# A feed-forward block by seven half products in place of eight

## The chip, the core and the metric

One NeuronCore of a Trainium2 chip runs the whole program. The metric is the device time of one execution in microseconds (us). The kernel is written in Python with one instruction stream for each engine: TensorE (PE, matmuls), VectorE (DVE), ScalarE (ACT), GpSimd (POOL) and SyncE (SP, which issues the transfers).

## The reference

Three residual blocks, one behind the other, on an input of 1024 rows and 1024 columns in fp32. The change touches the second block's end and the third block. The end of the second:

```python
    x = x + jnp.concatenate([y_rwkv, y_conv], axis=-1) @ w_out[l]
    h = rmsnorm(x, norm_mlp_g[l])
    x = x + jnp.square(jax.nn.relu(h @ w_ff1[l])) @ w_ff2[l]
return rmsnorm(x, norm_final_g)
```

`w_ff1` has 1024 x 4096 elements, `w_ff2` 4096 x 1024. The third block, cut to its products:

```python
proj = rms_norm_3(x, g_pre) @ w_in
u_a, v_a, z_a, q_b, k_b, v_b, z_b, gate_a, gate_b = jnp.split(proj, SPLIT_OFFS, axis=-1)
y_a = spatial_gating(jax.nn.gelu(u_a), jax.nn.gelu(v_a), ln_g, ln_b, w_s, b_s) * jax.nn.silu(z_a)
y_b = mixture_of_dilations(q_b, k_b, v_b) * jax.nn.silu(z_b)
m = sigmoid(gate_a + b_gate[:1024]) * (y_a @ w_pa) + sigmoid(gate_b + b_gate[1024:]) * (y_b @ w_pb)
return x + rms_norm_3(m @ w_o, g_post)
```

## The kernel before

**Split products.** Every fp32 operand of a matmul is split into a high part and the rest (`split`, L179: an ACT copy for the high part at L183, a DVE subtraction for the low one at L184), and each product is three matmuls, high by high, high by low and low by high (`mm3`, L255, the matmul at L261; with a tile of weights or of activations on the stationary side, 512 columns moving). A unit of weights is loaded into a buffer of the pool `wp` and split there (`wunit`, L222). Activations stand transposed in halves of 512 rows (`act_half`, L193), in slots of a ring of six buffers of 32 KB per partition.

**The feed-forward** (`feed_forward`, L1679). The hidden width of 4096 is cut into 16 units of 256. `first` makes a unit's hidden values for 512 rows at a time, 24 matmuls for 128 hidden columns, relu on ACT, square and split; `second` (L1705) multiplies a unit by its 256 rows of `w_ff2` and adds the 1024 x 1024 result into `xm` in SBUF (L1711 on DVE). Each layer has 16 x 96 = 1536 matmuls of 512 columns. The hidden values never leave SBUF. Beside the last units the final norm of the second block (`rms_rows`, L1666) and the first of the third (`rms_T`, L197) run tile by tile, then `vb_proj` begins.

**Seven products** (`Seven`, L1728). In the third block a 1024 x 1024 product of activations with a unit of 256 columns is taken as a 2 x 2 matrix of blocks by 2 x 2 blocks of weights, with seven block products in place of eight and sums ahead and behind. `sums` (L1744) makes the sums of activation blocks in four steps, each with four additions of high and low part (L1753) and four further operations (L1755 to L1758), all on POOL; `last_sum` (L1764) splits the fourth. `run` (L1779) goes through the units: four loads of 256 KB of raw weights, three differences of weights on POOL (L1795, the tile T), seven splits into tiles w (eight buffers, five products ahead), twelve matmuls per product (L1813) into the PSUM tags a, b and d, and five additions on DVE (L1835 to L1846). Its users are 16 `Gated` units and 8 `Gate` units. A Gated unit's `prepare` (L2118 to L2128) loads and normalizes v and loads the tile ws; its `begin` transposes ws on PE (L2133).

**Order.** A scheduler sets the order of each engine's instructions from the program's order, priorities and the pools' buffers; pools that stand at the same addresses in SBUF make the later one's first writer wait for the earlier one's last reader. SP issues all transfers, in one queue. `weave` and `woven` take turns between generators; `wunit_in` (L241) loads the tail's first weights `wx` while the last Gate units run. In the tail (`merge`, L2201) `from_b` makes the second product, `from_a` the first.

Of the kernel before, what the change touches and what calls it, by code (L numbers as in the profile page):

```python
# [55 lines left out]
class Ctx:  # L56
# [184 lines left out]
    def wunit_in(self, p, a, new):  # L241

        nc = self.nc
        hi, lo = (p.tile([128, 8, 256], R, name=self.nm("wx")) for _ in range(2))
# [1434 lines left out]
def feed_forward(c, X, xm, p):  # L1679

    nc, ins = c.nc, c.ins
    w1, w2 = ins["w_ff1_2"][0], ins["w_ff2_2"][0]
    unit = lambda u: slice(256 * u, 256 * u + 256)
    act = {}

    def first(u, W, hf):
        hs = slice(512 * hf, 512 * hf + 512)
        ah, al = act[u]
        for i in range(2):
            q = c.cm(W, slice(128 * i, 128 * i + 128), X, hf)  # L1690
            r = p.tile([128, 512], F32, tag="fr", name=c.nm("fr"), bufs=1)
            nc.scalar.activation(r, q, AF.Relu)
            nc.vector.tensor_tensor(r, r, r, op=OP.mult)
            c.split(ah[:, i, hs], al[:, i, hs], r)
            yield

    def load1(u):
        act[u] = tuple(p.tile([128, 2, 1024], R, tag=t, name=c.nm(t), bufs=2) for t in ("ah", "al"))
        return c.wunit([w1[:, unit(u)]])

    W = [load1(u) for u in range(2)]
    for hf in range(2):
        for u in range(2):
            yield from first(u, W[u], hf)
    def second(u, W, tiles):  # L1705
        for t in tiles:
            for nh in range(2):
                q = c.psum("mm")
                ns = slice(512 * nh, 512 * nh + 512)
                c.mm3(q, act[u], W, slice(128 * t, 128 * t + 128), ns, [(0, 0), (1, 1)])  # L1710
                nc.vector.tensor_tensor(xm[t][:, ns], xm[t][:, ns], q, op=OP.add)  # L1711
            yield

    load2 = lambda u: c.wunit([w2[unit(u), :]], ktiles=2)
    for u in range(14):
        yield from second(u, load2(u), range(8))
        W = load1(u + 2)
        for hf in range(2):
            yield from first(u + 2, W, hf)

    W = [load2(u) for u in (14, 15)]
    for hf in range(2):
        for u in range(2):
            yield from second(14 + u, W[u], range(4 * hf, 4 * hf + 4))

class Seven:  # L1728
# [15 lines left out]
    def sums(self, tmp):  # L1744
# [3 lines left out]
        self.s4 = tmp.tile([128, 4, 512], F32, name="sum4")  # L1748
        for k in range(4):
            v = {}  # L1750
            for n, (h, l) in ((21, self.A21), (22, self.A[4]), (11, self.A[1]), (12, self.A[2])):
                v[n] = tmp.tile([128, 512], F32, tag="v%d" % n, name=c.nm("v"), bufs=1)
                TT(v[n], h[:, k].bitcast(F32), l[:, k].bitcast(F32), op=OP.add)  # L1753
# [16 lines left out]
    def load(self, u, p):  # L1770

        c, nc = self.c, self.c.nc
        r = p.tile([128, 4, 4, 128], F32, tag="raw", name=c.nm("raw"), bufs=2)
        a, b = u.parts
        for i, (w, k) in enumerate(((a, 0), (b, 0), (b, 1), (a, 1))):
            nc.sync.dma_start(r[:, i], w[512 * k:512 * k + 512].rearrange("(k p) n -> p k n", p=128))
        return r

    def run(self, units, rp, p, st):  # L1779
        c, nc = self.c, self.c.nc  # L1780
        N = len(units)
        order = [(0, 1), (0, 2), (0, 6)]
        for n in range(N):
            order += [x for x in ((n, 2), (n, 5), (n, 7), (n + 1, 1), (n, 4), (n + 1, 6), (n, 3)) if 0 < x[0] < N or n == x[0] and x[1] != 2]
        for u in units[:1]:
# [716 lines left out]
```

## Time and profile before

| | |
|---|---|
| median of 3 runs | 3922.23 us (3918.51 to 3922.97) |
| the profiled execution | 3905.47 us |
| its span, first to last instruction | 3903.7 us |
| PE busy | 3718.5 us, 95% |
| DVE busy | 2178.6 us, 56% |
| ACT busy | 1316.1 us, 34% |
| POOL busy | 803.4 us, 21% |
| moved by DMA | 354.14 MB, mean 91 GB/s |

Busy shares are means over the span. The clock is the one granted to TensorE, as a share of full speed. An idle time of an engine other than the one that sets the end costs nothing. "L261" is line 261 of the kernel above.

### The profile page before, as it was taken

To read this page: it belongs to the slowest core of one execution; us is meant where nothing else is said; L and a number is where in the kernel's file an instruction comes from. 1 tells how busy PE (TensorE), PEld (TensorE's weight loads), DVE (VectorE), ACT (ScalarE), POOL (GpSimd) and SP (SyncE) were. 2 spreads that over 40 slices of the span, in tenths; PEclk is the share of its full clock that TensorE was granted. 3 is DMA by queue.
4 is the path that set the end of the run, shared out by engine and by line. 5 is a ranking of instruction groups with operands and counts; after the bars stand their busy time and mean duration, and the time that the engine had idled before them with its cause. 6 is when DMAs were issued, how large, how long until landed. Compare 5 with 4: busy or idle time off the path is not lost.

```text
span 3903.7 us, 53217 instructions
## 1 busy us (share of the span) xinstructions
PE 3718.5 (95%) x20000; PEld 3076.6 (79%) x20000; DVE 2178.6 (56%) x4701; ACT 1316.1 (34%) x2683; POOL 803.4 (21%) x1161
## 2 busy tenths in 40 slices
PE   7999999799979989999999999999989999998998
PEld 6788788687867778888888878878777888887887
DVE  5356568768977855444444644444442666544443
ACT  4444435642234334221122233333321333332322
POOL 1011124400048620000000001111150655420000
PEclk9999998899989999999999999999999999999999
DMA  5321242341212232111111132111122333337462
GB/s 148 126 64 51 73 148 70 128 134 60 89 56 52 62 113 92 54 54 44 45 53 44 71 107 66 44 49 55 49 96 86 93 102 105 102 119 249 152 228 94
DMA packets 362948, 354.14 MB, mean 91 GB/s; under 512 B 54014, under 2 KB 288322, under 8 KB 362690
## 3 DMA queue, kind: packets, MB, share of 16 engines
q1 hardware_dynamic: 362690, 350.73, 28.5%
q8 instruction: 158, 2.59, 0.3%
q14 instruction: 100, 0.82, 0.1%
HBM read 263.63 MB, written 82.31 MB: 89 GB/s over the span
## 4 chain that ended last, share of the span: by engine, by line
PE 83%; DVE 5%; POOL 4%; DMA 4%; ACT 2%; issue 1%; SPq 1%; DVEq 0%; POOLq 0%; ACTq 0%
PE mm L261 57%; PE b L1813 5%; PE d L1813 3%; PE a L1813 3%; PE s L1964 2%; DMA wraw<-in_w_in_dram 1%; PE s L542 1%; PE t L578 1%; PE o L1986 1%; DVE ws L748 1%; PE s L2156 1%; PE o L2038 1%; POOL v L1753 1%; PE t L213 1%; PE o L588 1%
## 5 line engine op out<-in xcount | busy, mean ns | idle before, releaser
L261 PE MATMUL mm<-ahi,whi 128*128 128x512 f32 x1936 | 762.4, 395 | 12.6 <-ACT whi L183 11.6
L261 PE MATMUL mm<-alo,whi 128*128 128x512 f32 x1936 | 760.6, 393 | 1.6 <-DVE alo L218 1.6
L261 PE MATMUL mm<-ahi,wlo 128*128 128x512 f32 x1936 | 759.1, 393 | 2.5 <-DVE wlo L184 2.5
L183 ACT ACTIVATE whi<-wraw 128x1024 fp32r<-128x1024 f32 (+2 forms) x266 | 268.7, 1055 | 671.2 <-DMA wraw<-in_w_ff_dram 320.9
L184 DVE TENSOR_TENSOR wlo<-wraw,whi 128x1024 fp32r<-128x1024 f32 (+2 forms) x266 | 322.0, 1247 | 257.5 <-PE mm L261 198.9
L261 PEld LDWEIGHTS mm<-ahi,whi 128*128 128x128 f32 x1936 | 366.9, 190 | 90.1 <-issue 12.4
L261 PEld LDWEIGHTS mm<-ahi,wlo 128*128 128x128 f32 x1936 | 365.8, 189 | 78.7 <-DVE wlo L184 3.3
L261 PEld LDWEIGHTS mm<-alo,whi 128*128 128x128 f32 x1936 | 366.4, 189 | 76.6 <-DVE alo L218 2.5
L261 PE MATMUL mm<-whi,ahi 128*128 128x512 f32 (+2 forms) x960 | 351.6, 371 | 31.8 <-ACT go L2097 10.9
L261 PE MATMUL mm<-wlo,ahi 128*128 128x512 f32 (+2 forms) x960 | 352.1, 367 | 0.0
L261 PE MATMUL mm<-whi,alo 128*128 128x512 f32 (+2 forms) x960 | 350.5, 366 | 1.6 <-DVE alo L218 1.6
L1711 DVE TENSOR_TENSOR xm<-xm,mm 128x512 f32<-128x512 f32 x256 | 173.9, 686 | 119.0 <-PE mm L261 118.6
L261 PEld LDWEIGHTS mm<-whi,ahi 128*128 128x128 f32 x960 | 183.8, 192 | 63.9 <-ACT go L2097 12.2
L261 PEld LDWEIGHTS mm<-wlo,ahi 128*128 128x128 f32 x960 | 183.8, 191 | 30.2 <-issue 3.8
L261 PEld LDWEIGHTS mm<-whi,alo 128*128 128x128 f32 x960 | 183.1, 191 | 31.0 <-issue 2.5
L261 PE MATMUL mm<-whi,ah 128*128 128x512 f32 x512 | 202.3, 395 | 0.0
L261 PE MATMUL mm<-wlo,ah 128*128 128x512 f32 x512 | 202.1, 395 | 0.0
L261 PE MATMUL mm<-whi,al 128*128 128x512 f32 x512 | 202.1, 395 | 0.0
L207 POOL TENSOR_SCALAR x<-x,rT 128x1024 f32<-128x1024 f32 x16 | 20.9, 1306 | 753.9 <-PE mm L261 672.9
L1813 PE MATMUL b<-sum,w 128*128 128x512 f32 x576 | 147.1, 398 | 0.2 <-DVE w L184 0.2
L1180 DVE SCALAR_TENSOR_TENSOR cva<-cvh,vecs,cva 128x1022 f32<-128x1022 f32 (+29 forms) x120 | 145.4, 1262 | 0.2
L560 POOL TENSOR_SCALAR S<-S,sn 128x64 f32<-128x64 f32 (+8 forms) x96 | 56.5, 592 | 382.6 <-DVE sn L558 158.2
(623 smaller groups left out, 6900.3 us busy)
## 6 DMA issues: line engine op xcount, KB each, us to landing
wraw<-in_w_in_dram SPq DMA_DIRECT2D x33, 1024.0 KB
wraw<-in_w_ff_dram SPq DMA_DIRECT2D x32, 1024.0 KB
wraw<-in_w_out_dram SPq DMA_DIRECT2D x24, 1024.0 KB
raw<-in_w_in_dram SPq DMA_DIRECT2D x96, 256.0 KB
wraw<-in_w_proj_a_dram SPq DMA_DIRECT2D x16, 1024.0 KB
wraw<-in_w_in_dram SPq DMA_DIRECT2D x27, 512.0 KB
gv<-go SPq DMA_DIRECT2D x32, 256.0 KB
vl<-gv SPq DMA_DIRECT2D x16, 512.0 KB
```

The lines of the kernel that those rows point to most:

```text
L183: nc.scalar.activation(hi, src, AF.Copy)
L184: nc.vector.tensor_tensor(lo, src, hi.bitcast(F32), op=OP.subtract)
L213: nc.tensor.transpose(q[:, 128 * j:128 * j + 128], xn[:, (k + j) * 128:(k + j + 1) * 128], self.ident)
L261: nc.tensor.matmul(out, lhs[a][:, kl, ls], rhs[b][:, kr, rs], start=first and n == 0, stop=last and n == tot - 1)
L542: nc.tensor.matmul(q[:, :b - a], self.Q[0:64, h, qs], kl, start=False, stop=True)
L560: nc.gpsimd.tensor_scalar(S_[:, :n], S_[:, :n], r, 1.0, op0=OP.mult, op1=OP.mult)
L578: nc.tensor.transpose(t[:w, (2 * j + s) * 128:(2 * j + s + 1) * 128], Ps[s][:, k:k + w], c.ident)
L588: nc.tensor.matmul(o[:, :256], v[:w, 0:128], ph[:w, sl], start=first, stop=last, skip_group_check=True)
L1180: nc.vector.scalar_tensor_tensor(a[:, 30 - j:], h[:, 0:994 + j], wj, a[:, 30 - j:], op0=OP.mult, op1=OP.add)
L1711: nc.vector.tensor_tensor(xm[t][:, ns], xm[t][:, ns], q, op=OP.add)
L1813: nc.tensor.matmul(o, w[:, i, k], self.A[P][j][:, k], start=P in (1, 6, 5) and m == 0, stop=m == 11, skip_group_check=True)
L1964: nc.tensor.matmul(q[:, :256], qk[:, a, qcol], qk[:, b, kcol], start=n == 0, stop=n == 2)
```

## The change

The feed-forward is rewritten and takes both layers by seven block products (units 0 and 1 of the first layer by eight, `EIGHT = 2`). A hidden unit's four blocks (11, 12, 21, 22: half of the rows by half of the columns) come out of `Seven`; the class `Hidden` squares them, makes five sums on POOL and writes the seven operands (the five sums and the blocks 11 and 22) to `hS` in DRAM, 256 KB each. The class `Second` reads these and blocks of `w_ff2` back, 512 KB at a time, makes the sums of weights on POOL and takes the seven products in four groups, (5, 7), (4, 1), (3, 6) and (2), each in eight steps of 24 matmuls per product, accumulating in PSUM. At the end of a group the results are added to `C`, four tiles of 1024 columns per half, into which the residual was loaded from `xmid` in DRAM, where `rows` had stored it. The last group is woven with the first four tiles' norms.

`Seven` is cut into `plan`, `load`, `make`, `product`, `by_eight` and `run`, and the activation sums' first additions may run on DVE (`both=True`). In the third block the plan and the first loads stand ahead of `v_proj`, two splits are made within it, the transposes of ws are kept in program order, and a second unit of `from_b` runs on the PSUM tag a before the pools of the tail open.

```diff
-def feed_forward(c, X, xm, p):
...
-    def sums(self, tmp):
+    def sums(self, new, both=False):
 
         c, nc = self.c, self.c.nc
         TT = nc.gpsimd.tensor_tensor
+        T0 = nc.vector.tensor_tensor if both else TT
...
-                TT(v[n], h[:, k].bitcast(F32), l[:, k].bitcast(F32), op=OP.add)
+                T0(v[n], h[:, k].bitcast(F32), l[:, k].bitcast(F32), op=OP.add)
...
+    def by_eight(self, p):
+
+        c, e = self.c, self.eight
+        for i, (n, hf, col) in enumerate(self.order[:4 * e]):
+            while self.made < min(4 + 2 * i, 4 * e) or self.made < min(2 * i, 4 * e + 5):
+                self.make(p)
...
+            A = ((self.A[1], self.A[2]), (self.A21, self.A[4]))[hf]
+            for kh in range(2):
+                self.product(o, self.W[n, (col, kh)], A[kh], kh == 0, kh == 1)
+            self.units[n].result(hf, col, o)
+            yield
...
+class Hidden:
+
+    SUMS = {1: (11, 22, OP.add), 2: (21, 22, OP.add), 5: (11, 12, OP.add), 6: (21, 11, OP.subtract), 7: (12, 22, OP.subtract)}
...
+    def out(self, m, x):
+        self.c.nc.sync.dma_start(self.hS[m - 1, 128 * self.n:128 * self.n + 128], x)
+
+    def result(self, hf, col, x):
+        c, nc = self.c, self.c.nc
+        me = 11 + 10 * hf + col
+        if me == 11 or self.n < EIGHT:
+            o = self.new(me)
+            nc.scalar.activation(o, x, AF.Relu)
+            nc.vector.tensor_tensor(o, o, o, op=OP.mult)
+        else:
+            o = x
+            nc.vector.scalar_tensor_tensor(o, x, 0.0, x, op0=OP.max, op1=OP.mult)
+        self.x[me] = o
+        if me in (11, 22):
+            self.out({11: 3, 22: 4}[me], o)
+        for m, (a, b, op) in self.SUMS.items():
+            if m not in self.done and a in self.x and b in self.x:
+                self.done.add(m)
+                t = self.sc.tile([128, 512], F32, tag="sc", name=c.nm("sc"), bufs=4)
+                nc.gpsimd.tensor_tensor(t, self.x[a], self.x[b], op=op)
+                self.out(m, t)
...
+class Second:
...
+    def parts(self, group, s, tp):
...
+        for m in group:
+            for x in self.B[m][:2]:
+                if x not in B:
+                    i, j = x // 10 - 1, x % 10 - 1
+                    B[x] = self.raw(self.w2[i][:, 2 * s:2 * s + 2, 512 * j:512 * j + 512])
+        for m in group:
+            A = self.raw(self.hS[m - 1, 256 * s:256 * s + 256].rearrange("(k p) n -> p k n", p=128))
+            o = out[m] = c.slot([128, 4, 2, 512], R, "fop")
+            c.split(o[:, 0], o[:, 1], A)
+            b = B[self.B[m][0]]
+            if len(self.B[m]) > 1:
+                t = tp.tile([128, 2, 512], F32, tag="ft", name=c.nm("ft"), bufs=2)
+                nc.gpsimd.tensor_tensor(t, b, B[self.B[m][1]], op=self.B[m][2])
+                b = t
+            c.split(o[:, 2], o[:, 3], b)
+        return out
...
+            seven.plan(units, rp, [(w7, 6), (w2p, 2)], eight=EIGHT)
+            tt = enter("T")
+            first = seven.by_eight(tt)
+            weave([(islice(first, 4), 4), (staggered(map(tile, range(4, 8)), 2), 10)])
...
+            weave([(first, 4), (seven.sums(four, both=True), 12)])
+            seven.last_sum()
+            for _ in seven.run(tt, st):
+                pass
+        with pool("f4") as f4, pool("ft") as tp, pool("fe") as ep:
+            c.set_banks(mm=list(range(8)))
+            sec = Second(c, hS, w2)
+            with pool("f4x") as fx:
+                sec.raws = [(f4, 5)] * 5 + [(fx, 10)] * 10
+                C = []
+                r = sec.run([(5, 7), (4, 1), (3, 6)], tp, ep, C)
...
+                weave([(sec.run([(2,)], tp, ep, C), 8), (norms[0], 12)])
+                X.append(c.act_half())
+                weave([(islice(vb, 8), 8), (norms[1], 12)])
...
+                for i, _ in enumerate(woven([(b.v_proj(X, vp, new), 16), (seven.sums(lambda: [tmp.tile([128, 512], F32, tag="v%d" % i, name=c.nm("v")) for i in range(4)]), 12)])):
+                    if i == 24:
+                        seven.make()
+                        seven.make()
...
-            nc.tensor.transpose(q[:, 0:128], self.ws, c.ident)
+            c.tc.keep_in_program_order(nc.tensor.transpose(q[:, 0:128], self.ws, c.ident))
...
-                for _ in b.from_b(0, 0, first[0], Ab, "a", new):
-                    pass
+                w = c.slot([128, 2, 8, 256], R, "wx")
+                first.append(c.wunit_in((w[:, 0], w[:, 1]), c.ins["w_proj_b_3"][0][:, 256:512], new))
+                for u in range(2):
+                    for _ in b.from_b(u, 0, first[u], Ab, "a", new):
+                        pass
```

Line numbers in the rows of the order are those of the kernel they stand in. First SP, in the middle of the feed-forward before: a unit's weights per load, first and second layer in turn, each 1 MB.

```order
L233 DMA wraw_2965_16353<-in_w_ff2_2_dram 128x2x1024
L233 DMA wraw_2986_16491<-in_w_ff1_2_dram 128x8x256
L233 DMA wraw_2997_16619<-in_w_ff2_2_dram 128x2x1024
L233 DMA wraw_3018_16757<-in_w_ff1_2_dram 128x8x256
L233 DMA wraw_3029_16885<-in_w_ff2_2_dram 128x2x1024
```

SP after the change, where the second layer begins: sc are sums of the last hidden units on their way to DRAM, f4 the buffers that the second layer loads, numbered in the order of the program.

```order
L2431 DMA f4_3217_18067<-hS_14680 128x2x512
L2390 DMA hS_14680<-sc_3212_18019 128x512
L2431 DMA f4_3219_18074<-hS_14680 128x2x512
L2431 DMA f4_3222_18083<-in_w_ff2_2_dram 128x2x512
L2390 DMA hS_14680<-sc_3213_18036 128x512
L2390 DMA hS_14680<-sc_3214_18039 128x512
L2431 DMA f4_3250_18242<-hS_14680 128x2x512
L2431 DMA f4_3253_18299<-in_w_ff2_2_dram 128x2x512
L2431 DMA f4_3254_18301<-in_w_ff2_2_dram 128x2x512
L2431 DMA f4_3255_18303<-hS_14680 128x2x512
L2431 DMA f4_3223_18085<-in_w_ff2_2_dram 128x2x512
L2431 DMA f4_3224_18087<-hS_14680 128x2x512
```

Stores and loads of hS share the queue, and four loads of a later step (3250 to 3255) stand ahead of two of the second step (3223, 3224).

POOL after the change, where the activations' sums are made: v and sum4 belong to `sums`, sc is a sum of hidden blocks (hid and ug).

```order
L1708 TENSOR_TENSOR v_2903_15802<-v_2903_15802 128x512
L2409 TENSOR_TENSOR sc_2902_15789<-hid_2901_15786,ug_2851_15478 128x512
L1709 TENSOR_TENSOR v_2903_15802<-v_2904_15803,v_2903_15802 128x512
L1710 TENSOR_TENSOR v_2904_15803<-v_2903_15802,v_2904_15803 128x512
L2409 TENSOR_TENSOR sc_2909_15843<-ug_2851_15478,hid_2908_15839 128x512
L2409 TENSOR_TENSOR sc_2910_15846<-hid_2901_15786,hid_2908_15839 128x512
L2409 TENSOR_TENSOR sc_2911_15849<-hid_2869_15570,hid_2908_15839 128x512
L1711 TENSOR_TENSOR sum4_15754<-v_2904_15803 128x512
```

Eight such hidden sums stand between the sixteen operations of `sums`; the four additions ahead of each step are not among POOL's rows.

PE where the third block's units begin, before: the end of `v_proj` (mm), the transpose of ws, the matmul by ones, then the first product of the first unit.

```order
L261 MATMUL mm_4601_26083<-wlo_4583_25884,ahi_3351_19547 128x512
L261 MATMUL mm_4601_26083<-whi_4582_25883,alo_3352_19548 128x512
L2133 MATMUL s_4635_26322<-ident_72,ws_4608_26193 128x128
L2137 MATMUL s_4637_26326<-wt_4636_26324,ones_74 128x128
L1813 MATMUL a_4622_26243<-ahi_3349_19545,w7_4612_26207 128x512
```

And after the change, at the end of the second product of the first unit:

```order
L1788 MATMUL a_4720_26573<-ahi_3457_19863,w7_4696_26356 128x512
L1788 MATMUL b_4728_26614<-sum_4597_25390,w7_4713_26547 128x512 x2
L1788 MATMUL d_4731_26636<-sum_4596_25389,w7_4714_26550 128x512 x2
L1788 MATMUL b_4728_26614<-sum_4597_25390,w7_4713_26547 128x512 x10
L1788 MATMUL d_4731_26636<-sum_4596_25389,w7_4714_26550 128x512 x10
L2135 MATMUL s_4733_26652<-ident_72,ws_4710_26539 128x128
L1788 MATMUL a_4742_26694<-ahi_3457_19863,w7_4716_26556 128x512
```

The first transpose of ws has moved from ahead of the first product to behind the fourth.

## Rows read from the trace of the kernel before

**Rows 1.** The cores: span and mean granted clock.
```profile
core 0: 3903.7 us, clock 0.971
```

**Rows 2.** Stretches of the feed-forward: us; busy PE, PEld, DVE, ACT, POOL; clock, DMA, GB/s.
```profile
1554.00:2224.00 670.00, 670.00 (x2920) 548.28 (x2920) 323.54 (x465) 139.63 (x195) 1.12 (x1) 1.00 0.16 50
2224.00:2290.00 66.00, 64.42 (x304) 52.63 (x303) 51.73 (x193) 36.00 (x97) 9.98 (x7) 0.97 0.29 106
```

**Rows 3.** The chain of waits in the feed-forward: start, us, what.
```profile
1553.76 669.83 PE mm L261 x2915
```

**Rows 4.** The chain of waits in the third block's units, two Gated, two Gate.
```profile
3065.13 5.59 PE b L1813 x24
...
3086.82 5.60 PE b L1813 x24
...
3405.72 2.80 PE a L1813 x12
...
3425.27 2.80 PE a L1813 x12
```

**Rows 5.** The stretch of the Gated units.
```profile
3065.00:3390.00 325.00, 325.00 (x1542) 267.61 (x1541) 203.00 (x289) 112.52 (x197) 174.77 (x179) 1.00 0.35 104
```

**Rows 6.** Stretches in which PE stood idle.
```profile
2830.00:2850.00 20.00, 10.78 (x40) 8.04 (x41) 8.76 (x20) 3.91 (x8) 10.09 (x15) 0.77 0.34 108
...
3020.00:3065.00 45.00, 43.37 (x186) 34.61 (x186) 25.02 (x35) 15.21 (x28) 30.79 (x35) 0.90 0.28 80
...
3540.00:3560.00 20.00, 8.60 (x32) 7.08 (x33) 8.99 (x8) 7.23 (x9) 0.00 (x0) 0.74 0.73 250
```

**Rows 7.** Waits of PE in the third block: total, times, longest.
```profile
PE mm L261 <- ACT whi L183: 11.6, 1, 11.6
...
PE s L2133 <- DMA ws<-in_w_spatial_dram: 4.2, 1, 4.2
...
PE a L1813 <- DVE w L184: 1.1, 1, 1.1
```

**Rows 8.** Groups beside the Gate units: busy, mean ns, idle before.
```profile
L1795 POOL TENSOR_TENSOR T<-raw,T 128x512 f32<-128x512 f32 x12 | 15.9, 1327 | 0.9
...
L1795 POOL TENSOR_TENSOR T<-raw 128x1024 f32<-128x1024 f32 x6 | 14.4, 2395 | 81.4 <-DVE w L184 81.4
L184 DVE TENSOR_TENSOR w<-raw,w 128x512 fp32r<-128x512 f32 x18 | 12.4, 687 | 2.2 <-ACT w L183 2.0
```

**Rows 9.** Groups of the feed-forward.
```profile
L1711 DVE TENSOR_TENSOR xm<-xm,mm 128x512 f32<-128x512 f32 x243 | 165.2, 686 | 118.8 <-PE mm L261 118.6
...
L184 DVE TENSOR_TENSOR wlo<-wraw,whi 128x1024 fp32r<-128x1024 f32 x60 | 70.9, 1222 | 43.3 <-PE mm L261 43.3
L183 ACT ACTIVATE whi<-wraw 128x1024 fp32r<-128x1024 f32 x60 | 60.2, 1052 | 319.9 <-DMA wraw<-in_w_ff_dram 318.4 <-DMA wraw<-in_w_in_dram 1.5
```

**Rows 10.** Two stretches with much DMA: the first block, the tail.
```profile
480.00:500.00 20.00, 20.00 (x110) 17.08 (x110) 4.53 (x18) 5.80 (x15) 1.45 (x3) 1.00 0.76 178
...
3520.00:3540.00 20.00, 19.80 (x86) 15.64 (x84) 11.24 (x12) 8.26 (x9) 0.00 (x0) 1.00 0.88 295
```

**Rows 11.** The same split as in rows 8, beside the Gated units.
```profile
L184 DVE TENSOR_TENSOR w<-raw,w 128x512 fp32r<-128x512 f32 x46 | 47.6, 1035 | 0.4
```

**Rows 12.** The chain through the activations' sums in the third block.
```profile
2843.16 4.96 POOL v L1753 x4
2848.12 1.24 POOL v L1755
...
2854.11 5.45 POOL v L1753 x4
...
2889.00 0.64 ACT sum L183
```

**Rows 13.** The chain at two waits for loads of 512 KB.
```profile
772.01 4.72 DMA alo<-mixT
...
3534.74 6.20 DMA alo<-yaT
```

More of the change, by code (lines that the diff above doesn't have):

```diff
@@ L239, in wunit, with wunit_in @@
                 lo[:, :ktiles * n].rearrange("p (k n) -> p k n", k=ktiles))
-    def wunit_in(self, p, a, new):
+    def wunit_in(self, w, a, new):
         nc = self.nc
-        hi, lo = (p.tile([128, 8, 256], R, name=self.nm("wx")) for _ in range(2))
+        hi, lo = w
         for k in range(0, 8, 2):
@@ L1676, in rms_rows @@
     yield
-def feed_forward(c, X, xm, p):
[L1681 to L1724, printed above, removed]
 class Seven:
@@ new lines, in make, with more_places @@
+        place = self.places[self.made % 8]
+        w = self.W[n, P] = place.tile([128, 2, 4, 128], R, tag="w7", name=c.nm("w7"), bufs=self.many[id(place)])
+        c.split(w[:, 0], w[:, 1], src)
+        if n < self.eight:
+            if P == (1, 1) and n + 2 == self.eight:
+                self.load(self.eight)
+        elif P == 3 and n + 2 < len(self.units):
+            self.load(n + 2)
+        self.made += 1
+    def more_places(self, p, n):
+        self.places += [p] * n
+        self.many[id(p)] = n
@@ new lines, in product @@
+    def product(self, o, w, A, first, last):
+        m = 0
+        for k in range(4):
+            for i, j in ((0, 0), (0, 1), (1, 0)):
+                self.c.nc.tensor.matmul(o, w[:, i, k], A[j][:, k], start=first and m == 0, stop=m == 11,
+                                        skip_group_check=True)
+                m += 1
+    def by_eight(self, p):
[3 more added lines that the diff above has]
+                self.make(p)
+            if hf == 0 and col == 0:
+                self.units[n].prepare()
+            o = c.psum("abd"[i % 3])
+            A = ((self.A[1], self.A[2]), (self.A21, self.A[4]))[hf]
[3 more added lines that the diff above has]
+            yield
@@ L1805, in use, with run @@
+    def run(self, p, st):
+        c, nc = self.c, self.c.nc
+        units, order, W, e = self.units, self.order[4 * self.eight:], self.W, self.eight
+        N = len(units)
+        self.load(e + 1)
+        units[e].prepare()
+        q, v = {}, {}
+        TT = nc.vector.tensor_tensor
         def use(n, P):
@@ L2079, in mod, with v_proj @@
             yield
-    def v_proj(self, X, p, tmp):
+    def v_proj(self, X, p, new):
         c, nc = self.c, self.c.nc
@@ L2436, in third_block @@
                 first = []
-                new = lambda: st.tile([128, 512], F32, tag="ug", name=c.nm("ug"), bufs=2)
                 def early():
                     tail.close()
-                    first.append(c.wunit_in(tail.enter_context(pool("wb")), c.ins["w_proj_b_3"][0][:, 0:256], new))
-                units = [b.Gated(b, g, st, p) for g in range(16)] + [b.Gate(b, n, st, early if n == 2 else None) for n in range(8)]
-                for _ in seven.run(units, rp, wp, st):
+                    hi, lo = (tail.enter_context(pool(t)).tile([128, 8, 256], R, name=c.nm("wx")) for t in ("wbh", "wbl"))
+                    first.append(c.wunit_in((hi, lo), c.ins["w_proj_b_3"][0][:, 0:256], new))
+                for u in units[:16]:
+                    u.p = p
+                units[18].when = early
+                for _ in seven.run(wp, st):
                     pass
```

237 lines of the change are left out of this document (160 added, 77 removed).

## The prediction

> **What bounds the kernel now.** I read the clock line first [rows 1]: mean 0.971, so TensorE stood at its upper level (2.4 GHz) nearly throughout. Next the table of stretches, for the stage that the change rewrites [rows 2]: in the feed-forward PE is busy 670.00 of 670 us at clock 1.00, VectorE (DVE) 323.54, the DMA engines 16%. The chain of waits says the same [rows 3]: one piece of 669.83 us and 2915 matmuls, 0.2298 us each, with nothing between them. So a matmul left out there is worth its whole 0.2298 us, as long as what replaces it stays hidden. Whether it does can be read from the one stage that already multiplies by seven products, the Gated and Gate units of the third block. The first matmuls of two following Gate units stand 19.55 us apart, those of two Gated units 21.69 us, a matmul there is 2.80/12 = 0.2333 us [rows 4], and PE is busy 325.00 of 325 us with DVE at 203.00 and POOL (GpSimd) at 174.77 [rows 5]. PE is idle in three places that the change touches: ahead of the third block's v projection, at its first Gated unit, and behind its last Gate unit [rows 6]. The waits name causes for the last two [rows 7]: 4.2 us for ws and 1.1 us for a split weight, and 11.6 us for the first weight of the tail.
>
> **The matmuls.** Before: 2 x 1536 = 3072, times 0.2298 = 705.9 us. After: the first layer has 2 units by eight (192 matmuls x 0.2333 = 44.8) and 14 by seven, each 84 matmuls like a Gate unit (14 x 19.55 = 273.7), the second layer 7 x 8 x 24 = 1344 x 0.2298 = 308.8. Sum 627.3, so PE's own time falls by 78.6 us. (360 fewer matmuls at 0.2298 would be 82.7; the rest is the longer matmul of the seven products.)
>
> **First layer, steady state.** The unit is a Gate unit with other results. POOL gets three differences of weights (2.395 + 2 x 1.327) and five sums (some 1.33 each, the same shape): 11.7 us of 19.55. DVE gets seven splits (7 x 0.687), five additions (0.686 each) and squares: some 11.5 us [rows 8, 9]. Raw weights (1 MB) and seven stores of 256 KB are 2.8 MB in 19.55 us, 145 GB/s, against 295 GB/s with PE at 19.80 of 20 [rows 10]. Forecast: hidden, cost 0; without that cover a unit costs what a Gated one does, 2.14 us more, 30 us in all.
> The two engines do get in each other's way: the split that takes 0.687 us beside Gate units takes 1.035 beside Gated ones, where POOL is busier [rows 8, 11]. The Trainium skill, "SBUF — State Buffer" (section "SBUF: two separate sides"), goes further: a DVE operation with two SBUF inputs and a GpSimd operation that reads SBUF exclude each other for their whole length. If so, a unit's 11.7 us of POOL and the 7.8 us of its DVE operations of that kind (seven splits, and four squares taken like the additions, 0.7) would fill 19.5 of 19.55 us, no slack at all; that is the supply rival below. The Gated row speaks against a loss: 203.00 + 174.77 exceeds 325, and PE lost nothing.
>
> **Start of the first layer.** The sums of activations move here: DVE takes the four additions per step, POOL keeps four per step and gets eight of the new hidden sums between them (order, POOL). In the third block POOL needs 5.99 us for the four and 4.96 for the additions, and the whole job ran 46 us, from 2843.16 to 2889.00 [rows 12]. Here POOL has 4 x 5.99 + 8 x 1.33 = 34.6 us; PE has 96 matmuls of the by-eight half and 24 of the first two products that need no sum, 28 us. Not covered: 0 (other order) to 18 us (46 - 28); I take 5, near 34.6 - 28, since POOL starts a little ahead.
>
> **Hand-over to the second layer.** SP issues all transfers in order. The order shows hS stores of the last unit, which wait for POOL's sums, ahead of the first hS loads, and the second step's loads (f4_3223, f4_3224) behind four for a later step. 512 KB took 4.72 and 6.20 us to land [rows 13]. From the last sum: a store and a load in series, then two splits of 1.05 and 1.22 us [rows 9]; PE has left only the last products, two of 2.80 us. Bounds 0 and 20 (two landings one behind the other, 12.4, splits, and a spell at half clock as in [rows 6], last); I take 8, one landing plus splits.
>
> **Second layer, steady state.** A step of two products has 48 matmuls, 11.0 us. ACT does 4 x 1.05, DVE 4 x 1.22, POOL at most 2 x 2.395 [rows 8, 9]: hidden. Loads: 128 x 524 KB = 67.1 MB in 308.8 us, 217 GB/s (up to five loads per 11.0 us, 238), against two stretches of [rows 10]: 295 at a DMA share of 0.88, and 178 at 0.76, that is 234 while the engines were busy. Both suffice for 217, the lower one just: cost 0, bound +27 us (67.1 MB at 200 GB/s is 335.5). Changes of group (three, results by ACT, DVE, POOL): 1 us in all, bounds 0 and 6. Product 2 is woven with four tiles' norms: DVE has 16 splits (19.6), 8 additions (5.5) and at most half of the 51.73 us that the stretch of the old norms shows [rows 2], 51 against PE's 44.1: I take 5, bounds 0 and 10. The first vb unit behind it, whose weights load into a pool that opens late: 2, bounds 0 and 6. The residual's eight stores and two loads lie beside PE: 0.
> Sum of losses 5 + 8 + 1 + 5 + 2 = 21; feed-forward net 78.6 - 21 = 58 gained.
>
> **Third block.** Early weight loads and two early splits take away the 1.1 us; the 24 matmuls that now stand ahead of the first transpose cover the 4.2 us for ws (order, PE). The stretch lost 1.6 us of PE and about 4.5 us of clock (0.10 of 45) beside that [rows 6]. Gain 5, bounds 0 and 11. Behind the last Gate unit, one more unit of from_b (48 matmuls, 11.2 us) runs while the tail's first weight loads: of the 11.6 us idle plus 5 us of clock (0.26 of 20) I take 11 back, bounds 0 and 17. The first gap (9.2 us idle, [rows 6]) stays: v_proj's weights wait for the same pool, and the sums' operations on POOL are not touched. Together 16.
>
> **Sum.** -58 - 16 = -74. The profiled execution took 3905.5 us, 1.8 over its span, and lies 16.8 below the median of the runs; 3905.5 - 74 = 3831, and on the median **3848 us**.
>
> **Rivals.**
> *Everything hides* (hand-overs covered, tail at its bound): -78.6 - 27 = -105, 3817. For it: each cover is within 20% of its need. Against: five hand-overs must all succeed, and each old one of this kind left 5 to 17 us [rows 6].
> *Supply binds a steady stage*: units at the Gated pace (+30), or loads at 200 GB/s (+27): about 3877. For it: [rows 11] and 178 GB/s in [rows 10]. Against: PE 325.00 of 325 in [rows 5].
> *Slower.* The second layer's 128 loads run one behind another, because SP's single queue holds each behind a wait for a buffer that the step before frees. At 4.72 us each that is 604 us against 308.8, +295 - 74: 4143. It decides from (308.8 + 74)/128 = 2.99 us per load (175 GB/s). For it: one queue, one issuing engine, buffers for about three steps; 178 GB/s in [rows 10]. Against: 295 GB/s there can't be reached by transfers that do not overlap. The Trainium skill, "DMA: Bandwidth & Descriptors" (sections "Anatomy of one DMA" and "Bandwidth"), asks for transfers of at least 1 MiB and puts a fixed 2.0 us on each; by its fit a lone 512 KB load would be an estimated 3.2 us, and this rival about 3949. The rows' 4.72 and 6.20 us are longer than that estimate.
> *No change*: the losses eat the gain, as when sums and hand-over stand at their upper bounds (+25), loads at 200 GB/s (+27), and the third block gives nothing (+16): 3848 + 68 = 3916. That the change leaves no matmul out is excluded by the order: 17213 in place of 17573.
>
> **How the numbers follow.** Forecast 0.62, everything hides 0.13, supply 0.14, no change 0.04, slower 0.07. The forecast's own range, from the bounds of the single losses half spent, is 3825 to 3870. With the neighbours on both sides the range for 8 in 10 is 3812 to 3890. A measurement of this kernel tells 0.2% (8 us) from no change; so faster 0.62 + 0.13 + 0.14 = 0.89, same 0.04, slower 0.07.
>
> **What would show it.** Right: in the new profile the by-seven units stand 19.5 to 19.6 us apart, with PE busy all of it; the second layer's steps 11.0 us; one gap each before the third product of the first by-seven unit (5 us, released by the sums) and at the second layer's start (8 us, released by an hS load); third block: no wait for ws, the tail's first weight wait short. Wrong: second-layer steps above 11.5 us with PE waiting for f4 loads (supply, or the slow rival above 12.9); units at 21 us or more with splits at 1 us (shared access); or a gap over 20 us at the hand-over, which would be SP's order.

## The result, and the profile after the change

The changed kernel takes 3849.17 us (median of 4 runs, 3844.50 to 3855.08) beside 3920.37 before; the ratio is 0.9828, 95% interval 0.9808 to 0.9847. Its profiled execution took 3849.69 us. The interval leaves out 1, so the change is faster by some 70 us. The page of that execution, busy time by engine:

```profile
span 3848.0 us, 53607 instructions
...
PE 3649.3 (95%) x19640; PEld 3018.1 (78%) x19640; DVE 2324.7 (60%) x4669; ACT 1385.6 (36%) x2777; POOL 1167.2 (30%) x1355
```

PE's busy time fell by 69 us, DVE's rose by 146 and POOL's by 364. The stretches of the new feed-forward (columns as in rows 2):

```profile
1580.00:1600.00 20.00, 15.70 (x48) 10.75 (x47) 20.00 (x16) 5.82 (x10) 16.75 (x11) 0.74 0.25 92
1600.00:1620.00 20.00, 9.21 (x17) 5.22 (x18) 13.75 (x14) 4.72 (x7) 11.06 (x8) 0.55 0.26 83
...
1640.00:1875.00 235.00, 235.00 (x1016) 190.80 (x1014) 174.98 (x192) 61.86 (x107) 155.92 (x96) 1.00 0.43 147
1875.00:1892.00 17.00, 6.73 (x27) 5.21 (x27) 7.31 (x9) 2.92 (x3) 8.62 (x6) 0.80 0.60 213
1892.00:2166.00 274.00, 274.00 (x1202) 226.66 (x1202) 204.51 (x140) 117.55 (x126) 139.02 (x55) 0.99 0.74 257
```

Both long stretches keep PE as full as [rows 2] did: 0.232 us per matmul that starts in it in the first layer (1014), 0.228 in the second. What is lost lies between them. From 1580 to 1620 PE started 64 matmuls in 40 us (the one across 1600 stands in both rows): 40 - 64 x 0.2298 = 25.3 us lost. Of these PE sat idle 15.1 us, by the rows' busy times; the other 10 us are matmuls that took longer, at a mean granted clock of 0.74 and 0.55, so part of them at the lower level (1.2 GHz). From 1875 to 1892, where 26 matmuls start, it is 17 - 26 x 0.2298 = 11.0 us. The waits of PE in the feed-forward name both:

```profile
PE mm L2471 <- ACT fop L183: 9.5, 1, 9.5
PE b L1788 <- DVE sum L184: 5.8, 3, 3.2
PE b L1788 <- ACT sum L183: 4.5, 2, 4.0
PE t L213 <- POOL x L207: 2.6, 1, 2.6
```

The first loss waits for sums of activations (L184 and L183 writing sum), the second for the second layer's first operand (fop).

To compare stages, the executions are cut at the end of the last matmul of the second block's recurrence (L1604 in both), the start of the last copy of vb, the start of the last yb and the end. Two profiles of each kernel (the second ones are the last two runs below), in us:

| stage | before | before, again | change | change, again |
|---|---|---|---|---|
| start to L1604's end (not touched) | 1450.9 | 1458.7 | 1454.2 | 1452.2 |
| to the last vb: output product, feed-forward, vb | 889.1 | 888.4 | 846.2 | 843.2 |
| to the last yb: attention (not touched) | 499.1 | 501.3 | 494.2 | 496.9 |
| to the end: v, units, tail | 1064.7 | 1069.8 | 1053.4 | 1053.3 |

By means the feed-forward stage gains 44 us, the third block's end 14, attention 5, the rest 2: 64 us in all.

### The profile page after: what moved, and what is told of

The parts are those of the page before. It is cut to its first block, busy times and chain, and to the rows that moved or that the text cites. A ratio compares the mean times of both kernels' runs of the same rounds, so it can differ in the third digit from the quotient of the medians.

```text
span 3848.0 us, 53607 instructions
## 1 busy us (share of the span) xinstructions
PE 3649.3 (95%) x19640; PEld 3018.1 (78%) x19640; DVE 2324.7 (60%) x4669; ACT 1385.6 (36%) x2777; POOL 1167.2 (30%) x1355
## 4 chain that ended last, share of the span: by engine, by line
PE 80%; DVE 6%; DMA 5%; POOL 4%; issue 2%; ACT 2%; SPq 1%; DVEq 0%; POOLq 0%; ACTq 0%
PE mm L261 40%; PE b L1788 8%; PE mm L2471 7%; PE a L1788 5%; PE d L1788 5%; PE s L1966 2%; DMA wraw<-in_w_in_dram 1%; PE s L542 1%; PE t L578 1%; PE o L1988 1%; PE s L2158 1%; PE o L2040 1%; DVE ws L748 1%; PE t L213 1%; PE o L588 1%
## 5 line engine op out<-in xcount | busy, mean ns | idle before, releaser
L261 PE MATMUL mm<-ahi,whi 128*128 128x512 f32 x1408 | 555.6, 396 | 2.2 <-issue 1.9
L261 PE MATMUL mm<-alo,whi 128*128 128x512 f32 x1408 | 553.5, 393 | 1.3 <-DVE alo L218 1.3
L261 PE MATMUL mm<-ahi,wlo 128*128 128x512 f32 x1408 | 552.5, 393 | 0.9 <-DVE wlo L184 0.9
L184 DVE TENSOR_TENSOR wlo<-wraw,whi 128x1024 fp32r<-128x1024 f32 (+2 forms) x200 | 244.6, 1256 | 192.4 <-PE mm L261 130.3
L2471 PE MATMUL mm<-fop 128*128 128x512 f32 x1344 | 310.7, 393 | 9.5 <-ACT fop L183 9.5
L183 ACT ACTIVATE whi<-wraw 128x1024 fp32r<-128x1024 f32 (+2 forms) x200 | 202.3, 1056 | 325.7 <-DMA wraw<-in_w_in_dram 101.6
L261 PEld LDWEIGHTS mm<-ahi,wlo 128*128 128x128 f32 x1408 | 265.8, 189 | 56.5 <-DVE wlo L184 2.1
L261 PEld LDWEIGHTS mm<-alo,whi 128*128 128x128 f32 x1408 | 266.2, 189 | 55.0 <-DVE alo L218 1.8
L2471 PEld LDWEIGHTS mm<-fop 128*128 128x128 f32 x1344 | 254.4, 190 | 63.0 <-ACT fop L183 9.9
L1788 PE MATMUL a<-ahi,w 128*128 128x512 f32 x656 | 223.8, 403 | 0.7 <-ACT r L1835 0.7
L1788 PEld LDWEIGHTS b<-sum,w 128*128 128x128 f32 x912 | 172.1, 191 | 54.4 <-DVE sum L184 7.3
L184 DVE TENSOR_TENSOR w<-T,w 128x512 fp32r<-128x512 f32 x152 | 142.2, 943 | 78.7 <-ACT w L183 78.4
```

Source lines behind the costliest of these rows:

```text
L183: nc.scalar.activation(hi, src, AF.Copy)
L184: nc.vector.tensor_tensor(lo, src, hi.bitcast(F32), op=OP.subtract)
L261: nc.tensor.matmul(out, lhs[a][:, kl, ls], rhs[b][:, kr, rs], start=first and n == 0, stop=last and n == tot - 1)
L1788: self.c.nc.tensor.matmul(o, w[:, i, k], A[j][:, k], start=first and m == 0, stop=m == 11, skip_group_check=True)
L2471: nc.tensor.matmul(q[m, t], o[m][:, a, k, 128 * t:128 * t + 128], o[m][:, 2 + b, k], start=s == 0 and n == 0, stop=s == 7 and n == 5)
```

## The experiments

**What each half of the change is worth.** `feed_forward` and `second_to_third` of the kernel before, with the change's third block.

```diff
+def feed_forward(c, X, xm, p):
...
 def second_to_third(c, pool, src, x2):
...
-            seven = Seven(c, H, s3)
...
+                ff = feed_forward(c, H, xm, fp)
```

> The old feed-forward with the new third block. The stage times of the two profiles put -45 us on the feed-forward and -11 us on the third block. Theory: the third block's part stands alone, so this kernel is 9 to 13 us faster than the kernel before, all of it at the first Gated unit and behind the last Gate unit. As forecast before the result it would be 16 us. Rival: the third block only gains because the feed-forward leaves it in another state (pools, queue), then within 3 us of the kernel before.

Measured 3898.82 us beside 3914.53 before, ratio 0.9956 (0.9941 to 0.9971). From the last yb to the end the profile has 1053.0 us, the change's own time, so the third block's part stands alone, and the rival (within 3 us) is out. Against the two profiles of before that is 12 and 17 us.

**What holds the first sums back.** The groups of DVE between 1556 and 1617 us of the change (busy, mean ns, idle before):

```profile
L184 DVE TENSOR_TENSOR sum<-v,sum 128x512 fp32r<-128x512 f32 x12 | 18.9, 1590 | 2.5 <-ACT sum L183 2.2
...
L2398 DVE TENSOR_TENSOR hid<-hid 128x512 f32<-128x512 f32 x5 | 6.7, 1335 | 1.0 <-ACT hid L2397 1.0
L184 DVE TENSOR_TENSOR w<-T,w 128x512 fp32r<-128x512 f32 x4 | 4.8, 1222 | 0.0
```

And those of POOL in the same stretch:

```profile
L2409 POOL TENSOR_TENSOR sc<-hid,hid 128x512 f32<-128x512 f32 x4 | 6.8, 1719 | 0.0
...
L1708 POOL TENSOR_TENSOR v<-v 128x512 f32<-128x512 f32 x4 | 6.1, 1518 | 8.2 <-DVE v L1706 8.2
```

The same subtraction of 128 x 512 took 0.687 us in [rows 8]; here it takes 1.59, and POOL's operations 1.5 to 1.7 for 1.33. The two engines take turns. Of DVE's 40 operations of 128 x 512 there that read two operands from SBUF, 19 take 0.68 us, and none of these begins while a POOL operation runs; the other 21 take 1.23 to 1.79 us, and each of them begins while one runs and ends 0.55 us behind it. One such pair (start, us, what):

```profile
1578.02 1.61 POOL L1709 TENSOR_TENSOR v<-v,v 128x512 f32<-128x512 f32 x1 [0.69 <-DVE v L1706]
...
1578.40 1.77 DVE L184 TENSOR_TENSOR sum<-v,sum 128x512 fp32r<-128x512 f32 x1
```

The second kernel changes one operand of eight DVE operations:

```diff
-            nc.vector.tensor_tensor(o, o, o, op=OP.mult)
+            nc.vector.tensor_tensor(o, o, x, op=OP.mult)
```

> The eight squares of the units by eight multiply relu(x) by x itself, which lies in PSUM, in place of relu(x) by relu(x): same count, same result, one operand in SBUF in place of two. Theory (DVE and POOL take turns when both read two operands from SBUF): each square falls from a mean of 1.3 us to 0.7 in that stretch, and PE's loss ahead of the first sums (25 us) shrinks by 4 to 9 us. Rival (the stretch is as long as POOL's own work on sums, whatever DVE reads): the squares may be shorter, the loss stays within 2 us.

3854.50 us, ratio to before 0.9846 (0.9829 to 0.9862), not told from the change. Its groups of DVE in that stretch, 1564 to 1626 us here:

```profile
L184 DVE TENSOR_TENSOR sum<-v,sum 128x512 fp32r<-128x512 f32 x12 | 18.6, 1563 | 2.5 <-ACT sum L183 2.2
...
L184 DVE TENSOR_TENSOR w<-T,w 128x512 fp32r<-128x512 f32 x4 | 5.5, 1396 | 0.0
...
L2398 DVE TENSOR_TENSOR hid<-hid,a 128x512 f32<-128x512 f32 x2 | 1.4, 682 | 1.0 <-ACT hid L2397 1.0
```

The theory was right on the squares, the rival on the loss. The squares fell from 1.335 to 0.68 us, so it is the second operand in SBUF that makes DVE wait for POOL. But the splits of the sums stayed at 1.56 us, those of the differences T rose from 1.222 to 1.396, and the loss only went from 25.3 to 23.9 us (40 us less 64 and 70 matmuls; the first layer from 348.3 to 346.0 us). The Trainium skill, "SBUF — State Buffer" (section "SBUF: two separate sides"), has this rule, that a DVE operation with two SBUF inputs and a GpSimd operation that reads SBUF exclude each other; this kernel agrees, 1.335 against 0.68 us for one operand moved.

So next the work of POOL itself was taken away: all 32 operations of `sums` on DVE.

```diff
-        TT = nc.gpsimd.tensor_tensor
-        T0 = nc.vector.tensor_tensor if both else TT
+        TT = nc.vector.tensor_tensor if both else nc.gpsimd.tensor_tensor
+        T0 = TT
```

> All 32 operations of the activation sums of the feed-forward on DVE, none on POOL; POOL keeps the hidden sums. Theory A (POOL's chain of 25 operations, 40 us busy, sets the start of the first layer): POOL is left with 9 operations, the loss of 25 us falls to 10 to 17. Theory B (DVE is the full engine there, 54 of 61 us): DVE gets 16 operations of 0.68 more and waits less for POOL, the loss stays within 5 us of 25 or grows.

3843.27 us, ratio 0.9808 (0.9791 to 0.9824). The first layer is 8.3 us shorter (340.0 us from its first to its last matmul, for 348.3); the loss is about 17 us, theory A's upper end. The interval of the timed runs overlaps that of the change, as those of the other single mends below do; what each is worth is read from the stages of its profile. The first layer of the change itself repeats to 0.3 us (348.0 in its second profile). DVE did 16 operations more in less time; its row for the same splits between 1558 and 1611 us:

```profile
L184 DVE TENSOR_TENSOR sum<-v,sum 128x512 fp32r<-128x512 f32 x12 | 9.3, 775 | 0.0
```

And a row of POOL's hidden sums there:

```profile
L2409 POOL TENSOR_TENSOR sc<-hid,ug 128x512 f32<-128x512 f32 x2 | 8.2, 4115 | 11.1 <-DVE hid L2398 11.1
```

So POOL's share of `sums` was worth 8 of the 25 us. Now DVE is the full engine (busy 49.7 of these 53 us), and POOL waits. The two operations of that row differ, though:

```profile
1575.05 6.49 POOL L2409 TENSOR_TENSOR sc<-hid,ug 128x512 f32<-128x512 f32 x1 [11.14 <-DVE hid L2398]
1581.50 1.74 POOL L2409 TENSOR_TENSOR sc<-ug,hid 128x512 f32<-128x512 f32 x1
```

While the first one stood, DVE ran eight operations on two SBUF operands one behind another, 0.68 us each; POOL's ended only after DVE had paused for 0.56 us.

Counted as one engine, an estimate with 1.33 us for POOL's operations, 0.68 for DVE's of 128 x 512 on two SBUF operands and 1.22 for its two of 128 x 1024, the work of that stretch is 25 x 1.33 + 40 x 0.68 + 2 x 1.22 = 63 us in the change, which took 61, and 9 x 1.33 + 56 x 0.68 + 2 x 1.22 = 52 here, which took 53. One rival mend was not tried: to put the eight hidden sums, which stand between those of `sums` on POOL, behind them.

**More cover in place of less work.** Four units by eight in place of two, in pairs:

```diff
-EIGHT = 2
+EIGHT = 4
...
-        E = [(n, hf, col) for hf in range(2) for n in range(eight) for col in range(2)]
+        E = [(n, hf, col) for j in range(0, eight, 2) for hf in range(2) for n in range(j, j + 2) for col in range(2)]
...
-            if P == (1, 1) and n + 2 == self.eight:
-                self.load(self.eight)
+            if P == (1, 1) and n + 2 <= self.eight:
+                self.load(n + 2)
```

> Four units by eight in place of two, taken in pairs. Theory (the sums need more PE work to hide behind, and the backlog of DVE and POOL is a fixed amount): the loss ahead of the first sums falls from 25 us to 3 or less, two units by eight cost 2 x 2.85 = 5.7 us more, net 16 to 20 us faster than the change. Rival (DVE and POOL are short of throughput for the whole first layer, so the backlog moves on): the wait turns up later, net between no change and 6 us slower.

3841.15 us, ratio 0.9812 (0.9798 to 0.9827), 8 us below the change by medians, 13.6 us by the profile from L1604's end, less than the 16 to 20 expected. The theory's mechanism holds: the backlog is a fixed amount, and PE now has work nearly throughout:

```profile
1560.00:1640.00 80.00, 78.83 (x343) 63.45 (x341) 73.44 (x72) 27.23 (x55) 58.70 (x35) 1.00 0.22 79
```

But one wait is left behind it, the longest of PE's in the first layer:

```profile
PE a L1788 <- ACT r L1836: 5.6, 1, 5.6
```

The chain leads through ACT, which waits for a load of raw weights to split; in the chain the load ends at 1643.86 us. Its buffer, one of two in turn, had been the fourth sum's. In the next kernel that sum and the terms v changed places:

```diff
-        self.s4 = self.rp.tile([128, 4, 4, 128], F32, tag="raw", name="sum4", bufs=2).rearrange("p a b c -> p a (b c)")
+            V, S = new()
+            self.s4 = S
...
+                V = rp.tile([128, 4, 4, 128], F32, tag="raw", name="v4", bufs=2).rearrange("p a b c -> p a (b c)")
```

> Four units by eight, and the fourth sum lies where the terms v lay and the terms v in the raw-weight buffer where the fourth sum lay, so that this buffer is free as soon as the sums are split. Theory (with four units the sums are covered, and the 6 us left ahead of the first product by seven are a load of raw weights that waits for this buffer): no wait above 1 us there, 5 to 7 us faster than four units alone, 13 to 20 us faster than the change. Rival (the load is late for another reason, SP's queue or the splits): the 6 us stay.

3841.37 us, ratio 0.9808 (0.9793 to 0.9823): a miss, by the profiles from L1604's end 4 us longer than four units alone. The wait for ACT is still there with 3.8 us, and two waits of 2.1 us for DVE came beside it. The buffer is free when DVE has split the last sum, and DVE got there hardly earlier; so it seems to be DVE that was late, not the buffer alone.

**The hand-over.** In the change the second layer's start looks like this in the chain of waits (start, us, what):

```profile
1878.85 2.81 PE d L1788 x12
...
1883.14 6.87 DMA f<-hS
...
1890.03 1.07 ACT fop L183
...
1891.14 69.02 PE mm L2471 x294
```

Although hS of the first step had long been written, its load is issued only when the last product ends. With four buffers in the first pool, at the place of the raw weights, it needs not wait for PE:

```diff
-                sec.raws = [(f4, 5)] * 5 + [(fx, 10)] * 10
+                sec.raws = [(f4, 4)] * 4 + [(fx, 11)] * 11
...
-            sec.raws = [(f4, 5)]
+            sec.raws = [(f4, 4)]
```

> The first pool of load buffers of the second layer has four places in place of five, so that it fills the place of the raw weights exactly and none of the first step's loads overlaps weights that PE still reads. Theory (SP's one queue stood behind a load that waited for the last products): the loss at the hand-over falls from 12 us to 4 or less, 8 to 11 us in all. Rival (a store, a load and two splits in series after the last product set it): the loss stays 10 us or more, as the first loads were not needed earlier.

3853.14 us, ratio 0.9838 (0.9821 to 0.9855), no gain. The first step now ran between the last products, from 1878.18 us on, ahead of their end at 1888.02; but PE then waited 10.5 us, in two pieces, as much as the rival said. The chain at the second:

```profile
1892.06 3.52 POOL sc L2409 x2
...
1895.61 3.09 DMA hS<-sc
...
1899.90 6.34 DMA f<-hS
...
1907.37 17.63 PE mm L2471 x69
```

The second step's loads stand in SP's queue behind a store of the last hidden sums; that store waits for POOL. The wait had moved by one step. So the second step's buffers went to the place of the third activation sum, free two products before the end (the expectation says three), and SP's order then has its loads ahead of the last stores:

```diff
-            with pool("f4x") as fx:
-                sec.raws = [(f4, 4)] * 4 + [(fx, 11)] * 11
+            with pool("f4x") as fx, pool("sp") as sp, pool("f4y") as fy:
+                sp.tile([128, 3616], F32, name="spacer")
+                sec.raws = [(f4, 4)] * 4 + [(fy, 4)] * 4 + [(fx, 7)] * 7
```

> As the kernel with four first load buffers, and the second step's four buffers moved to the place of the third activation sum, which is free three products before the first layer ends; SP then issues that step's loads ahead of the last stores of hidden sums. Theory (the loads of the second step stood in SP's queue behind stores that wait for the last sums, so the wait only moved by one step when the first step came early): no wait of PE at the hand-over or in the first three steps above 2 us, 7 to 10 us faster than the change. Rival (the transfers themselves can't come faster, whatever their order): PE still loses 7 us or more in the first four steps.

3843.98 us, ratio 0.9819 (0.9801 to 0.9837), 5 us below the change by medians; by the profiles both layers together are 11.5 us shorter, from first to last matmul (665.1 for 676.6). The theory holds in the main, but for waits of 4.7 us in all, the longest 2.5 where none above 2 was expected; the last comes from POOL, which now has sums of weights (ft) ahead of the last hidden sums (sc). The chain there:

```profile
1894.75 4.70 POOL ft L2450 x2
1899.45 4.47 POOL sc L2409 x2
...
1905.36 6.88 DMA f<-hS
```

**Depth of the loads, the slower rival's mechanism.** Six load buffers in place of fifteen:

```diff
-                sec.raws = [(f4, 5)] * 5 + [(fx, 10)] * 10
+                sec.raws = [(f4, 5)] * 5 + [(fx, 1)]
```

> Six load buffers in place of fifteen in the second layer: the case of the slower rival, loads that can't run ahead of the step before. By rows a batch of loads takes 6 us to land and 2.3 us to split against 11.0 us of PE for a step: theory (depth is what hides the single queue): steps of 12 to 15 us, the second layer 25 to 90 us longer. Rival (the queue keeps up anyway): under 8 us longer.

One run, 3845.32 us. The second layer lost nothing. Its stretch in this kernel (columns as in rows 2):

```profile
1890.00:2160.00 270.00, 268.97 (x1179) 222.57 (x1180) 198.53 (x139) 119.08 (x127) 133.20 (x56) 0.99 0.75 264
```

The same stretch of the change:

```profile
1890.00:2160.00 270.00, 268.86 (x1177) 222.44 (x1178) 199.39 (x133) 118.92 (x127) 140.18 (x56) 0.99 0.75 260
```

My expectation was far off, and the rival holds. By the code, what runs ahead are the split operands in the ring (six slots, of 16 KB each and not the 32 given for the kernel before; two for a step), not the raw loads: a load buffer is free as soon as it is split. That is argued; no run changed the number of slots. The change's wait of 2.6 us for the first norm also went; why was not tried.

**Joined.** Four units by eight, sums on DVE, squares with x from PSUM and the hand-over's buffers, once with the fifteen of it and once with 4 + 4:

```diff
-            with pool("f4x") as fx:
-                sec.raws = [(f4, 5)] * 5 + [(fx, 10)] * 10
+            with pool("sp") as sp, pool("f4y") as fy:
+                sp.tile([128, 10784], F32, name="spacer")
+                sec.raws = [(f4, 4)] * 4 + [(fy, 4)] * 4
```

> Joined: four units by eight, the sums on DVE, the squares with x from PSUM, and the load buffers of the second layer ordered as in the hand-over kernel (4 + 4 + 7). The parts gave, by their stages, 14 us (four units), 8 us (sums on DVE), 2 us (squares) and 11 us (hand-over); the first three act on one loss of 25 us, of which four units leave 8. Expected: 14 + 4 + 10 = 28 us faster than the change, at least 20. Rival (each part only moves the same backlog of DVE to another place): under 18 us.

> The same with eight load buffers in place of fifteen (4 + 4). Six buffers cost nothing in the run with few buffers, and with eight SP's order has the loads of steps two and three ahead of the last stores. Expected: 0 to 6 us faster than the joined kernel with fifteen, since less is fetched ahead of the last hidden sums on POOL. Rival (fifteen are needed across the changes of group): 2 to 10 us slower than it.

> The change itself again, beside the joined kernels and the kernel before, in the same rounds. By the medians of its first runs it gains 71 us, by the stages of the two profiles, counted from the end of the stage that the change does not touch, 59. Expected between: 58 to 72 us faster than the kernel before.

3822.62 us with fifteen, ratio 0.9757 (0.9740 to 0.9775), and 3819.29 with eight, 0.9748 (0.9732 to 0.9764), not told apart; the change again 3848.01, 0.9822 (0.9807 to 0.9837), before 3917.47, 69 us apart where 58 to 72 were expected. So the joined kernel with eight beats the change by 29 us in the same rounds, and the kernel before by 98. The stretches of the kernel with eight over the first sums and over the hand-over:

```profile
1533.60:1620.00 86.40, 86.33 (x388) 69.92 (x387) 73.46 (x124) 34.14 (x77) 34.03 (x20) 1.00 0.26 89
...
1860.00:1880.00 20.00, 15.30 (x59) 11.42 (x58) 13.24 (x11) 7.83 (x8) 12.81 (x6) 0.91 0.80 258
```

The first loss is gone; of the second 20 - 57 x 0.2298 = 7 us are left (57 of the 59 matmuls start in the stretch). With four units DVE has the time for the sums, which with two it had not. The 28 us expected came out as 25 with fifteen buffers and 29 with eight. The parts do not simply add up: singly four units, sums on DVE, squares and hand-over gave 14 + 8 + 2 + 11 = 35 us, and the first three act on one loss of 25. Which of the two small ones took away what four units had left was not tried apart.

**The kernel before again.**

> The kernel before itself, with a second profile. Its medians lie 9 to 15 us above the one profiled execution, from which the stages were counted (59 us gained by stages, 69 to 71 by medians). Theory: the difference lies in the two blocks ahead of the change, which took 1450.9 us in that profile and up to 1463.5 in others, and the stages from there on repeat within 2 us; then 59 us is what the change is worth in its own stages. Rival: the stages that the change rewrites were themselves short in that profile; then the feed-forward or the third block is 5 to 12 us longer in this one.

3915.17 us beside 3915.25. The second profile is 14.4 us longer than the first: 7.8 of it ahead of L1604's end, 1.5 to the last yb, 5.1 behind it; the feed-forward stage repeats to 0.7 us. So the theory holds for the feed-forward, and 10 of the 14.4 us lie in stages that the change doesn't touch; for the third block the rival holds: it varies by 5 us, at its first units and in the tail, and why is open.

## Why the prediction was right, and where not

The time, 3848 against 3849.2, is nearer than its working. Against the profile the sum said -74 us; the two first profiles differ by 56, the two second ones by 73. The step of adding the 16.8 us between profile and median made up for it: the one profile of before was a short execution, mostly in stages that the change doesn't touch, and the change's median lies where its profile does. That is luck: by means of two profiles the touched stages gave 58 us for the 74 of the sum (44 for 58, 14 for 16); some 6 more lie in stages without an edit, and the other 5 to 7 of the 69 to 71 between the medians in the scatter of single executions.

*The matmuls*: right. The first layer by seven runs at 0.232 us per matmul (forecast 0.2333) with PE busy all of 235 us, the second at 0.228 (forecast 0.2298). A slip that moves nothing: by its own prices a unit's seven splits and four squares are 7.6 us on DVE, not 7.8, and with five additions 11.0, not 11.5.

*Losses of the feed-forward*, forecast 21 us, net gain 58. Counted as time less 0.2298 us per matmul of 512 columns (0.11 per transpose):

| term | forecast | measured |
|---|---|---|
| start of the first layer | 5 (0 to 18) | 25.3 |
| hand-over | 8 (0 to 20) | 11.0 |
| product 2 and norms | 5 (0 to 10) | 4.3 |
| changes of group | 1 (0 to 6) | none seen |
| vb | 2 (0 to 6) | 5 gained: 6.1 us lost between 2250 and 2340 before, 1.0 between 2210 and 2301 after |
| output product | 0 | 2.7 |

78.6 less these is 40 with the 5 us gained, and the stage measured 42.9 by the first profiles; most of the rest is the shorter matmul of both layers.

The term that was mis-sized is the **start of the first layer**: "POOL has 4 x 5.99 + 8 x 1.33 = 34.6 us", set against 28 us of matmuls, gave 5 us, and it took 25.3. The stretch of the sums:

```profile
1556.00:1617.00 61.00, 45.84 (x164) 32.80 (x163) 53.61 (x59) 19.54 (x39) 40.14 (x25) 0.79 0.14 52
```

POOL's 25 operations took 40.1 us, and it sat idle some 20 of those 61 us, most of it waiting for DVE, whose operations on two SBUF operands stretched from 0.68 us to means of 0.95 to 1.59. From the first addition to POOL's last operation the job took 52 us (1561.1 to 1613.5), not 34.6. I had considered the exclusion of the two engines, but weighed it only for the steady stage, where "the Gated row speaks against a loss"; there PE indeed lost nothing, as the neighbours' waits are hidden. At the start nothing hides them. The cover was shorter, too: PE had matmuls that need no sum until 1584.7 us, 23.5 us behind the first addition, not 28. And the term had nothing for the clock: PE's 15.1 us of idle time lie within its bounds of 0 to 18, and it is the 10 us of slower matmuls that go beyond. The moved additions are of the kind that excludes POOL's; that was no reason to leave them on POOL, as the kernel with all sums on DVE shows.

*Hand-over*: the order of SP was the right place, the 8 us a little low (11.0). The first load waited for PE by its place in SBUF; the second step's loads, as the prediction said, for the stores. Both had to be mended before anything was gained.

*Supply and the slower rival*: wrong by a wide margin, as forecast. In the second layer the change moved up to 399 GB/s:

```profile
1892.00:1912.00 20.00, 20.00 (x82) 16.28 (x82) 11.81 (x10) 9.50 (x11) 5.21 (x2) 0.91 1.04 390
...
1900.00:1920.00 20.00, 20.00 (x90) 16.52 (x89) 16.04 (x9) 11.12 (x11) 11.55 (x4) 1.00 1.05 387
1920.00:1940.00 20.00, 20.00 (x90) 16.57 (x89) 14.19 (x11) 8.04 (x8) 6.29 (x2) 1.00 1.04 399
```

In the first row, 390 GB/s, the loads are all of 512 KB, many at once; two of 2 MB for the residual, issued at 1912.9 and 1914.1 us, share the other two. PE was busy throughout. The Trainium skill, "DMA: Bandwidth & Descriptors" (section "Bandwidth"), asks for 1 MiB or more, by transfers issued from GpSimd; these are issued from SP, and falling short of it cost nothing here, by these rows.

*Third block*: forecast 16, measured 11 by the first profiles, 16 by the second ones, 15.7 (11 to 23) by the timed run of that half alone. The first units went as forecast (6 us by means from the last yb to the first product, forecast 5), the tail gave 6 for 11, the units in between 2: in the tail PE still stands about 5 us, now with the chain running through a store of the added unit (8.16 us) to the tail's first weight:

```profile
3485.98 8.16 DMA mb<-ug
...
3495.10 9.01 DMA wraw<-in_w_proj_b_dram
```

Its stretches:

```profile
3480.00:3500.00 20.00, 17.41 (x69) 13.79 (x68) 9.27 (x11) 6.26 (x8) 0.00 (x0) 0.91 0.83 275
3500.00:3520.00 20.00, 17.62 (x70) 13.82 (x70) 11.47 (x12) 9.81 (x10) 0.00 (x0) 0.91 0.70 239
```

The 5 us that attention seems to gain stay open: no edit lies there, and profiles of one kernel differ by 2 to 3 us in it.

## What to carry to other kernels

Where a stage starts up, price DVE and POOL as one engine for all operations of POOL that read SBUF and all of DVE that read two operands from it, and count the cover from the moment the first operand is there. Then such an operation moved between the two is worth the difference of their prices: 0.68 us on DVE for 1.33 on POOL, 10 us for 16 operations by estimate, 8 measured. A few more matmuls to hide behind were the larger mend here (14 us), and with both, and the squares' operand in PSUM, the loss was gone. A wait of PE can cost more than its length: of the 25 us lost at the start 10 were matmuls at a lower granted clock. In an in-order queue look at what each load stands behind, step by step: freeing the first one only shows the second.

## What the runs showed of the hardware that was not expected

An operation of 1.33 us on POOL took 6.49 while DVE ran eight operations on two SBUF operands one behind another. It is a single one: the four that follow took 1.74 us each and alternated with DVE's, so when DVE keeps its turn is open. Loads of 512 KB from one queue moved 390 GB/s over 20 us with PE busy, more than the 295 of [rows 10]. And the same program's first 1450 us differed by 8 us between two profiles of the kernel before (1450.7 to 1463.5 over all profiles here): a gain read from two single profiles has at least that uncertainty.
